# Two-layer hybrid decoder trunk: first rows in a written order, two banks for each norm transpose, another order of the mixer's parts

## The chip, the cores and the metric

The kernel runs on one core of a Trainium2 chip. The metric is the device time of one execution in microseconds; the median of three runs is compared. Engines are named as in the profile: PE is TensorE (PEld its weight loads), DVE is VectorE, ACT is ScalarE, POOL is GpSimd, SP is SyncE, which here issues almost all DMAs.

## The reference, cut to what matters

Two layers, each of them three sublayers with a norm behind each. `mod` are nine rows of 1024 per layer that depend on `c` alone: shift, scale and gate for each sublayer.

```python
for l in range(DEPTH):                       # DEPTH 2, SEQ 256, D_MODEL 1024, D_FF 2816
    mod = (silu(c) @ ada_w[l] + ada_b[l]).reshape(b_, 3, 3, 1024)
    y = swiglu(modulate(x, mod[:, 0, 0], mod[:, 0, 1]), ffn_w13[l, 0], ffn_w2[l, 0])
    x = layer_norm(ALPHA * x + 0.5 * (1 + mod[:, 0, 2])[:, None, :] * y, ln_g[l, 0], ln_b[l, 0])
    y = token_mixer(modulate(x, mod[:, 1, 0], mod[:, 1, 1]), w_in[l], w_out[l], ...)
    x = layer_norm(ALPHA * x + (1 + mod[:, 1, 2])[:, None, :] * y, ln_g[l, 1], ln_b[l, 1])
    y = swiglu(modulate(x, mod[:, 2, 0], mod[:, 2, 1]), ffn_w13[l, 1], ffn_w2[l, 1])
    x = layer_norm(ALPHA * x + 0.5 * (1 + mod[:, 2, 2])[:, None, :] * y, ln_g[l, 2], ln_b[l, 2])
# token_mixer: h @ w_in, then three groups of heads of width 64 side by side, then @ w_out:
#   6 heads gated delta rule (GDN): conv + silu on q, k, v; unit q, k; a scan over 4 chunks of 64 tokens
#   4 heads MoBA (one block of 256 here, so plain causal softmax attention)
#   6 heads mLSTM: conv + silu on q, k; sigmoid output gate; a norm over each head
```

All inputs and the output are float32.

## The kernel before

**Numbers.** Each float32 operand of a large product is cut into a high part `hi` (rounded to fp32r, on ACT, line 101) and a low part `lo` (the difference, on DVE, line 104), and a product is three matmuls, `mm3` (lines 108 to 111): high by high, high by low, low by high. The activations are kept transposed as `xh` and `xl`, eight blocks of 128 columns by 256 tokens.

**Stages.** Six phases run in turn: FFN, mixer, FFN in layer 0, then the same in layer 1. An FFN (`ffn`) takes the 22 column blocks of `w13` two at a time, and then `out_rows` multiplies with `w2`; the products of its last four rows are held back (`held`) and issued within the norm. Between two phases stands `boundary`: gate, residual add, statistics and scaling of the norm on DVE, ACT and POOL, then for each half `t` of the tokens two calls of `turn`, which transpose four blocks of 128 columns on PE into one bank of PSUM; `mod` applies the next scale and shift, even columns on ACT and odd ones on DVE, and `high` and `low` cut the result. The first projection of the next phase (`product`) follows for each half. The planner that orders the instructions never lets two engines use one PSUM bank at a time. The `late` items are modulation columns whose last products wait for this place.

**Orders.** Three kinds of order matter. SP's queue, and so the order of nearly all loads, is the program order. `boundary` is written by hand for PE, DVE and ACT. All else is ordered by the planner, which works down the program order by what it takes to be ready; engines then run their queues strictly in order. `tc.issue_after(ins)` ties what is traced inside it to follow `ins` on the engine of `ins`.

**The first rows.** The first FFN has no boundary ahead of it. `first_rows` (lines 559 to 618) loads all of `x`, transposes it, and then for each of eight blocks k of 128 rows loads 128 columns of `ada_w` each for shift and scale of that block (rows of 512 bytes) and 128 rows of `w13` for seven column blocks. DVE sums the products of the `ada_w` block with `sc_` (line 595 and 597, eight steps), PE sums over partitions (line 599), two adds finish shift and scale, ACT and DVE make `xh`, `xm` and `xl`, and 42 matmuls per k add into seven banks. Six parameter loads and four transposes of them stand ahead (`param_columns`), on ACT's DMA queue.

**Background.** The other modulation rows come from `ada_block`: four chunks of `ada_w`, each with two DVE steps of 128x1024, put into a list `bg` that the FFNs work off between their weight chunks; with the fourth chunk `fin()` sums over partitions on PE.

**The mixer.** `mixer` projects q, k and v of GDN (`proj_T`, `conv_silu`, squares on POOL at line 771), runs GDN's steps as a generator `gd`, adds the residual rows of the coming norm (`state["residual"]()`, lines 514 to 520, two loads of norm rows and four DVE steps of 128x1024), projects the mLSTM parts and MoBA's, and then takes turns with the generators `ml` and `mo`. GDN is a scan; its solve of the triangular blocks runs on POOL (lines 976 and 978). `mix_T` transposes the finished columns: blocks 0 to 2 are GDN, 3 and 4 MoBA, 5 to 7 mLSTM. `out_rows` multiplies with `w_out` in the block order (3, 4), (0, 1), (2, 5), (6, 7). The mLSTM output gate (`mlstm_gate`, line 830) is one Sigmoid on ACT.

## Time and profile before

| | us |
|---|---|
| median of three runs | 1236.38 |
| lowest and highest | 1231.99, 1237.64 |
| the profiled execution | 1231.17 |
| its span, first to last instruction | 1229.5 |
| PE busy in it | 1160.3 (94%) |
| DVE busy | 894.8 (73%) |
| ACT busy | 578.4 (47%) |
| POOL busy | 107.2 (9%) |
| mean granted clock of PE | 0.975 |

The profile gives, for one execution, when each instruction ran, how long its engine had been idle ahead of it and what ended that idle time. Busy shares of a whole span are means over stages with different limits, so the stretches are read by themselves. Matmuls overlap in the pipeline: the distance between their starts is their pace, not the duration shown for one.

### The profile page before, as it was taken

What the parts mean: (1) busy time and instruction counts of PE and PEld (TensorE: products, weight loads), DVE (VectorE), ACT (ScalarE), POOL (GpSimd) and SP (SyncE); (2) the same over time, 40 slices, a digit from 0 to 9 for tenths busy, and PEclk for the clock granted to TensorE, in tenths of its full rate; (3) what the DMA queues carried; (4) which work ended last, traced back from release to release, by engine and by line L of the source; (5) the groups of instructions that cost most, each with busy time, mean ns of one, the idle gap of its engine ahead of it and who ended that gap; (6) DMA issues with size and microseconds to landing.
All of it is one profiled execution on the core that took longest, in us unless ns stands there. A gap on an engine that the chain in (4) does not pass through costs nothing.

```text
span 1229.5 us, 21037 instructions
## 1 busy us (share of the span) xinstructions
PE 1160.3 (94%) x8584; PEld 1051.4 (86%) x8584; DVE 894.8 (73%) x1423; ACT 578.4 (47%) x934; POOL 107.2 (9%) x174
## 2 busy tenths in 40 slices
PE   6899999988999799999999999999999979999996
PEld 4899988788997678999778999888898867999984
DVE  7889977677665679888578877776884766756655
ACT  3355443366573355544335554435755625544431
POOL 1000000012511200000000000001332120000001
PEclk9899999989998899999999999998999989999998
DMA  9999797363342159987638977671643431765650
GB/s 307 343 320 369 277 410 292 119 184 127 122 148 85 35 191 354 325 313 291 237 140 283 365 260 280 252 275 51 209 125 126 161 113 33 258 224 178 234 206 34
DMA packets 171522, 265.99 MB, mean 216 GB/s; under 512 B 5407, under 2 KB 136987, under 8 KB 171425
## 3 DMA queue, kind: packets, MB, share of 16 engines
q1 hardware_dynamic: 170368, 262.32, 62.1%
q10 hardware_dynamic: 1056, 2.32, 0.5%
q8 instruction: 67, 1.10, 0.4%
q14 instruction: 31, 0.25, 0.1%
HBM read 263.56 MB, written 1.06 MB: 215 GB/s over the span
## 4 chain that ended last, share of the span: by engine, by line
PE 77%; DVE 8%; DMA 5%; ACT 4%; POOL 3%; issue 2%; SPq 0%; DVEq 0%; ACTq 0%; POOLq 0%
PE pg L110 14%; PE pg L109 14%; PE pg L111 14%; PE pacc L109 9%; PE pacc L111 8%; PE pacc L110 8%; DMA raw<-in_ffn_w_dram 3%; DVE lo L104 2%; PE pg L225 1%; POOL xt L976 1%; POOL X L978 1%; ACT xm L450 1%; PE pg L233 1%; ACT hi L101 1%; DMA araw<-in_ada_w_dram 1%
## 5 line engine op out<-in xcount | busy, mean ns | idle before, releaser
L104 DVE TENSOR_TENSOR lo<-raw,hi 128x1024 fp32r<-128x1024 f32 (+3 forms) x332 | 396.4, 1200 | 163.4 <-PE pg L111 73.0
L101 ACT ACTIVATE hi<-raw 128x1024 fp32r<-128x1024 f32 (+4 forms) x352 | 353.9, 1027 | 294.8 <-DMA raw<-in_ffn_w_dram 113.3
L109 PE MATMUL pg<-xh,hi 128*128 128x256 f32 x1568 | 447.6, 287 | 5.4 <-ACT xh L604 2.7
L110 PE MATMUL pg<-xl,hi 128*128 128x256 f32 x1568 | 447.6, 286 | 1.5 <-DVE xl L607 1.5
L111 PE MATMUL pg<-xh,lo 128*128 128x256 f32 x1568 | 445.7, 285 | 0.0
L109 PEld LDWEIGHTS pg<-xh,hi 128*128 128x128 f32 x1568 | 301.9, 193 | 8.1 <-ACT xh L604 3.4
L110 PEld LDWEIGHTS pg<-xl,hi 128*128 128x128 f32 x1568 | 303.7, 194 | 3.4 <-DVE xl L607 2.0
L111 PEld LDWEIGHTS pg<-xh,lo 128*128 128x128 f32 x1568 | 303.2, 194 | 0.3
L260 DVE SCALAR_TENSOR_TENSOR adacc<-araw,sc__132,adacc 128x1024 f32<-128x1024 f32 x118 | 150.9, 1279 | 4.9 <-DMA araw<-in_ada_w_dram 4.1
L110 PE MATMUL pacc<-lo,hh 128*128 128x512 f32 x352 | 139.8, 397 | 1.6 <-DVE lo L104 1.5
L109 PE MATMUL pacc<-hi,hh 128*128 128x512 f32 x352 | 140.8, 400 | 0.0
L111 PE MATMUL pacc<-hi,hl 128*128 128x512 f32 x352 | 139.6, 396 | 0.0
L110 PEld LDWEIGHTS pacc<-lo,hh 128*128 128x128 f32 x352 | 66.3, 188 | 19.4 <-DVE lo L104 3.4
L109 PEld LDWEIGHTS pacc<-hi,hh 128*128 128x128 f32 x352 | 66.3, 188 | 16.4 <-issue 0.7
L111 PEld LDWEIGHTS pacc<-hi,hl 128*128 128x128 f32 x352 | 66.3, 188 | 15.9
L177 POOL TENSOR_TENSOR lsm<-lsm,mhalf 128x1 f32<-128x1 f32 x12 | 7.9, 660 | 701.1 <-DVE lsm L349 701.1
L632 ACT ACTIVATE sg<-pg 128x256 f32<-128x256 f32 x79 | 29.5, 375 | 81.2 <-PE pg L111 77.0
L639 ACT ACTIVATE hh<-h 128x256 fp32r<-128x256 f32 x82 | 33.8, 412 | 47.2 <-DVE h L634 46.8
L640 DVE TENSOR_TENSOR hl<-h,hh 128x256 fp32r<-128x256 f32 x82 | 34.4, 420 | 19.5 <-ACT hh L639 19.5
L109 PE MATMUL pacc<-hi,xh 128*128 128x512 f32 (+1 forms) x80 | 34.1, 427 | 10.2 <-ACT xh L454 10.2
L733 DVE SCALAR_TENSOR_TENSOR cy<-pg,cvc,cy 128x255 f32<-128x255 f32 (+2 forms) x90 | 40.1, 473 | 4.2 <-ACT cy L731 3.7
L339 ACT ACTIVATE lsq<-n,lsm 128x512 bf16<-128x512 f32 x24 | 17.3, 720 | 49.3 <-DVE lsm L328 31.5
(377 smaller groups left out, 1398.8 us busy)
## 6 DMA issues: line engine op xcount, KB each, us to landing
raw<-in_ffn_w_dram SPq DMA_DIRECT2D x118, 1024.0 KB, 5.7
araw<-in_ada_w_dram SPq DMA_DIRECT2D x64, 1024.0 KB, 8.6
raw<-in_w_in_dram SPq DMA_DIRECT2D x16, 1024.0 KB
araw<-in_ada_w_dram SPq DMA_DIRECT2D x16, 512.0 KB, 6.5
raw<-in_w_out_dram SPq DMA_DIRECT2D x8, 1024.0 KB, 4.8
raw<-in_ffn_w_dram SPq DMA_DIRECT2D x16, 448.0 KB, 6.1
raw<-in_ffn_w_dram SPq DMA_DIRECT2D x14, 512.0 KB, 4.5
raw<-in_w_in_dram SPq DMA_DIRECT2D x8, 792.0 KB, 6.7
```

The costliest lines, as they stand in the source:

```text
L101: state["hi"] = nc.scalar.activation(hi, v, AF.Copy)
L104: state["lo"] = nc.vector.tensor_tensor(lo[j], v[:, j * m:(j + 1) * m, :], hi[:, j * m:(j + 1) * m, :].bitcast(F32), op=ALU.subtract)
L109: nc.tensor.matmul(o, ah, bh, start=first, stop=False)
L110: nc.tensor.matmul(o, ah, bl, start=False, stop=False)
L111: nc.tensor.matmul(o, al, bh, start=False, stop=last)
L225: nc.tensor.matmul(pt[:, m:m + 1], acc[:, m * 128:(m + 1) * 128], ones[:, 0:1], start=True, stop=True)
L260: nc.vector.scalar_tensor_tensor(acc, raw[:, kk, :], sc_[:, k:k + 1], acc, op0=ALU.mult, op1=ALU.add)
L339: return nc.scalar.activation(sq[:, :c1 - c0], self.n[:, t, c0:c1], AF.Square, bias=self.cols(t, 6), accum_out=self.cols(t, 3 + h))
L632: nc.scalar.activation(sg, pa, AF.Silu)
L639: nc.scalar.activation(hh[:, f, :], h, AF.Copy)
L640: nc.vector.tensor_sub(hl[:, f, :], h, hh[:, f, :].bitcast(F32))
L733: nc.vector.scalar_tensor_tensor(y[:, s:], ps[:, :T - s], w(3 - s), y[:, s:], op0=ALU.mult, op1=ALU.add)
```

## The change

- `first_rows` gets a written order for PE, DVE and ACT. `ada_w` for block 0 is loaded first, then `x` in two halves of columns with `w13` 0 between, then `ada_w` 1, `w13` 1; blocks 2 to 7 of `ada_w` come in pairs (rows of 1 KB, in the tiles that later hold `hh` and `hl`). DVE sums five of the eight row blocks (seven for a pair) and PE the others. `xm` moves to ACT. The empty products that opened the banks are gone.
- Five of the six parameter loads go to SP and, with three transposes, into the second weight chunk of the first FFN.
- `ada_block`: `fin()` is a fifth item of the list; the gate's bias row is loaded by SP.
- `boundary`: each `turn` takes two banks, even columns in one and odd in the other; the late columns come after the transposes of the second half.
- `mixer`: two small copies (`gt`, `gi`) and the squares move to ACT, the residual goes behind the `mqk` projections, the gate becomes Exp, add and reciprocal and comes ahead of the mLSTM heads, MoBA's heads come after mLSTM's, and the output projection takes (3, 4) last.

```diff
 def param_columns():
+            column(rows[:72, 0, :], 72, abc[:, 0:72])
+            return lambda: more_param_columns(rows)
+        def more_param_columns(rows):
+            nc.sync.dma_start(rows[0:72, 1, :], ada_b[1].rearrange("(k p) -> k p", p=128))
...
+            for i, n, dst in ((1, 72, abc[:, 72:144]), (2, 96, lnc), (3, 120, cvc)):
                 column(rows[:n, i, :], n, dst)
 def ada_block(l, blk, pool, late=None):
-                            nc.scalar.dma_start(st["acc"][0:1, :], ada_b[l:l + 1, blk * 1024:blk * 1024 + D])
+                            nc.sync.dma_start(st["acc"][0:1, :], ada_b[l:l + 1, blk * 1024:blk * 1024 + D])
-                    if i == 3 and late is None:
-                        fin()()
-                    elif i == 3:
+                    if i == 3 and late is not None:
                         late.append(fin)
-            return [chunk(i) for i in range(4)]
+            return [chunk(i) for i in range(4)] + ([lambda: fin()()] if late is None else [])
 def boundary(l, s, acc, held, late, nx, sp, bp):
             def turn(t, q):
-                pts[t, q] = v = (ps_acc(1) if t else ps_g()).rearrange("p (a b) -> p a b", a=4)
+                pts[t, q] = v = [(ps_acc(1) if t and not q else ps_g()) for _ in range(2)]
                 for k in range(4):
-                    nc.tensor.transpose(v[:, k, :], nr.n[:, t, (4 * q + k) * 128:(4 * q + k + 1) * 128], ident)
+                    nc.tensor.transpose(v[k % 2][:, k // 2 * 128:k // 2 * 128 + 128],
+                                        nr.n[:, t, (4 * q + k) * 128:(4 * q + k + 1) * 128], ident)
...
             ps = [nx["product"](0, xh, xl)]
+            turn(1, 0)
+            turn(1, 1)
             if late:
                 pt = ps_g()
                 left = [fin(pt[:, i * 8:i * 8 + 8]) for i, fin in enumerate(late)]
-            turn(1, 0)
-            turn(1, 1)
 def first_rows(l, i, nf):
+            groups = {0: 1, 1: 1, 2: 2, 4: 2, 6: 2}
+            nv = {1: 5, 2: 7}
...
+            def mod_p(k):
+                n0 = nv[groups[k]]
+                for i in range(groups[k]):
+                    for j in range(2):
+                        o, sl = cps[:, 8 * j + k + i:8 * j + k + i + 1], slice(i * 128, (i + 1) * 128)
+                        for kk in range(n0, KD):
+                            nc.tensor.matmul(o, raws[k][:, kk, j, sl], sc_[:, kk:kk + 1], start=kk == n0, stop=False)
+                        nc.tensor.matmul(o, sums[k][:, j, sl], ones[:, 0:1], start=False, stop=True)
...
+            with tc.manual_schedule(engines={E.PE, E.DVE, E.Activation}):
+                load_mod(0), load_x(0), load_w(0), load_x(1), load_mod(1), load_w(1)
+                turn(0), turn(2)
+                mod_v(0, 0, nv[1])
+                mod_p(0), mod_c(0), apply(0)
+                ws = high(0)
+                low(0, 0, ws), low_x(0), low(0, 1, ws)
+                for k in range(KD):
+                    if k + 2 in groups:
+                        load_mod(k + 2)
+                    if k + 2 < KD:
+                        load_w(k + 2)
+                    now = ws
+                    if k + 1 < KD:
+                        ws = high(k + 1)
+                    if k == 0:
+                        products(0, 0, now[0], 0, nf - 2)
+                        products(0, 1, now[1], 0, nf - 2)
+                        turn(4), turn(6)
                     else:
+                        products(k, 0, now[0])
+                    if k + 1 in groups:
+                        mod_v(k + 1, 4 if groups[k + 1] > 1 else 0, nv[groups[k + 1]])
+                        mod_p(k + 1)
+                    if k + 1 < KD:
+                        low(k + 1, 0, ws)
+                        if k + 1 in groups:
+                            mod_c(k + 1)
+                        apply(k + 1)
+                        low(k + 1, 1, ws), low_x(k + 1)
+                    if groups.get(k + 2, 1) > 1:
+                        mod_v(k + 2, 0, 4)
+                    if k == 0:
+                        products(0, 0, now[0], nf - 2)
+                        products(0, 1, now[1], nf - 2)
+                    else:
+                        products(k, 1, now[1])
 def ffn(l, i, xh, xl, nx, first=None):
+                if not first and cc == 1:
+                    more_columns()
 def mixer(l, mp, xh, xl, pz):
-                nc.vector.tensor_copy(gt[:, t, :], pz[t][:, 0:12])
+                nc.scalar.activation(gt[:, t, :], pz[t][:, 0:12], AF.Copy)
-                    nc.gpsimd.tensor_mul(r, dst, dst)
+                    nc.scalar.activation(r, dst, AF.Square)
-            state["residual"]()
             mqk = mp.tile([128, 6, T], F32, tag="mqk", name="mqk")
...
             proj_T(2316, [(0, 1), (2, 3), (4, 5)], mqk_sink)
+            with tc.issue_after(state["silu"].ins):
+                state["residual"]()
...
             def mlstm_gate():
-                with tc.issue_after(state["exp"].ins):
-                    state["exp"] = nc.scalar.activation(state["so"], state["so"], AF.Sigmoid)
+                so = state["so"]
+                with tc.issue_after(state["after"]):
+                    nc.scalar.activation(so, so, AF.Exp, scale=-1.0)
+                nc.vector.tensor_scalar(so, so, 1.0, None, op0=ALU.add)
+                nc.vector.reciprocal(so, so)
...
             next(ml)
-            for _ in mo:
-                pass
+            mlstm_gate()
             next(ml)
-            mlstm_gate()
...
-            mix_T(mix, mh, mlo, [(3, 5, 0, 2)], ps_mb)
             mix_T(mix, mh, mlo, [(0, 3, 0, 1), (0, 3, 1, 2)], ps_d)
             for _ in ml:
                 pass
+            for _ in mo:
+                pass
             mix_T(mix, mh, mlo, [(5, 7, 0, 2), (7, 8, 0, 2)], ps_d)
+            mix_T(mix, mh, mlo, [(3, 5, 0, 2)], ps_mb)
...
-                    rest = end(*out_rows(lhs, w_out[l], [(3, 4), (0, 1), (2, 5), (6, 7)], nx))
+                    rest = end(*out_rows(lhs, w_out[l], [(0, 1), (2, 5), (6, 7), (3, 4)], nx))
```

## Rows read from the trace of the kernel before

**Rows 1.** The page, part 4: shares of the span on the chain by engine.

```profile
PE 77%; DVE 8%; DMA 5%; ACT 4%; POOL 3%; issue 2%; SPq 0%; DVEq 0%; ACTq 0%; POOLq 0%
```

**Rows 2.** Stretches: length, busy (instructions) of PE, PEld, DVE, ACT, POOL; PE clock, DMA share, GB/s.

```profile
22.50:74.00 51.50, 47.22 (x347) 46.72 (x348) 44.93 (x97) 22.39 (x27) 0.00 (x0) 0.93 1.05 332
74.00:223.00 149.00, 148.01 (x998) 135.03 (x997) 129.84 (x149) 66.33 (x97) 0.96 (x1) 1.00 0.90 330
80.00:90.00 10.00, 10.00 (x85) 10.00 (x85) 10.00 (x14) 6.33 (x11) 0.00 (x0) 1.00 0.97 356
```

**Rows 3.** What PE waited for: total us, times, longest us.

```profile
PE pgdn L301 <- DVE mix L1239: 11.9, 2, 6.0
PE pacc L109 <- ACT xh L454: 10.2, 10, 1.4
PE pm L773 <- POOL sq L771: 5.6, 4, 1.9
...
PE pg L233 <- DVE adacc L260: 2.5, 1, 2.5
```

**Rows 4.** Timeline of the first rows: start, us, instruction [idle before, what ended it].

```profile
10.71 0.35 DVE L595 TENSOR_SCALAR ada<-araw,sc__132 128x256 f32<-128x256 f32 x1 [4.21 <-DMA araw<-in_ada_w_dram]
...
17.64 0.95 ACT L101 ACTIVATE hi<-raw 128x896 fp32r<-128x896 f32 x1 [2.76 <-DMA raw<-in_ffn_w_dram]
...
22.53 0.58 PE L110 MATMUL pg<-xl,hi 128*128 128x256 f32 x1 [0.89 <-DVE xl L607]
...
54.38 0.95 ACT L101 ACTIVATE hi<-raw 128x896 fp32r<-128x896 f32 x1 [4.28 <-DMA raw<-in_ffn_w_dram]
...
73.85 0.64 ACT L632 ACTIVATE sg<-pg 128x256 f32<-128x256 f32 x2
```

**Rows 5.** Groups by line and shape: busy us, mean ns | idle before.

```profile
L104 DVE TENSOR_TENSOR lo<-raw,hi 128x896 fp32r<-128x896 f32 x16 | 17.4, 1089 | 2.6 <-PE pacc L111 2.2 <-issue 0.3
...
L604 ACT ACTIVATE xh<-xT,modc 128x256 fp32r<-128x256 f32 x8 | 4.8, 599 | 8.5 <-DVE modc L602 8.5
...
L597 DVE SCALAR_TENSOR_TENSOR ada<-araw,sc__132,ada 128x256 f32<-128x256 f32 x56 | 25.7, 479 | 0.4
```

**Rows 6.** Stretches with other row sizes of the loads, columns as in rows 2.

```profile
90.00:110.00 20.00, 20.00 (x168) 20.00 (x167) 19.70 (x26) 9.99 (x16) 0.00 (x0) 1.00 1.05 369
150.00:180.00 30.00, 30.00 (x197) 26.84 (x196) 25.93 (x32) 12.78 (x18) 0.00 (x0) 1.00 1.02 408
```

**Rows 7.** Timeline of the fourth boundary, DVE and PE.

```profile
834.18 0.41 DVE L448 TENSOR_SCALAR xm<-pg,sp,bp 128x128 f32<-128x128 f32 x1 [0.79 <-ACT xm L450]
...
839.08 0.45 PE L109 MATMUL pacc<-hi,xh 128*128 128x396 f32 x1 [1.05 <-ACT xh L454]
```

**Rows 8.** Timeline in the first mixer, ACT and DVE on two banks of `pg`.

```profile
387.45 0.28 ACT L1210 ACTIVATE nds<-pg 128x130 f32<-128x130 f32 x1 [2.62 <-PE pg L1209]
...
387.46 0.28 DVE L1204 SCALAR_TENSOR_TENSOR mP<-pg,Wx 128x128 f32<-128x128 f32 x1
```

**Rows 9.** Timeline at the start of the first mixer, DVE and ACT.

```profile
265.07 2.36 DVE L518 TENSOR_TENSOR xa<-n,gb 128x1024 f32<-128x1024 f32 x2 [0.52 <-DMA gb<-in_ln_g_dram]
...
271.68 2.00 ACT L101 ACTIVATE hi<-raw 128x1024 fp32r<-128x1024 f32 x2 [6.70 <-DMA raw<-in_w_in_dram]
```

**Rows 10.** Timeline at the end of the first mixer, PE.

```profile
415.09 1.09 PE L301 MATMUL pgdn<-ident,mix 128*128 128x128 f32 x4 [5.98 <-DVE mix L1239]
```

**Rows 11.** The stretch behind it, columns as in rows 2.

```profile
417.00:419.20 2.20, 2.20 (x7) 1.64 (x6) 0.44 (x2) 0.00 (x0) 0.00 (x0) 0.50 0.00 0
```

**Rows 12.** Timeline in the first mixer, MoBA's second pair of heads: first scores, last output.

```profile
376.44 0.79 PE L1250 MATMUL pmb<-bqk 64*128 64x128 f32 x2
...
386.46 0.74 DVE L1285 TENSOR_TENSOR mix<-pm,bsm 128x256 f32<-128x256 f32 x2
```

**Rows 13.** Two lines with a reciprocal: duration ns min/median/max, first and last start us, form.

```profile
L881 DVE RECIPROCAL be__2579<-be__2579 x1: 228/228/228, 256.5 to 256.5; 128x12 f32<-128x12 f32 x1
...
L1222 DVE RECIPROCAL mrd<-mrd x4: 180/182/182, 397.4 to 997.4; 128x6 f32<-128x6 f32 x4
```

126 lines of the change are left out of this document (69 added, 57 removed).

## The prediction

> **What bounds the kernel now.** I read the chain of waits first: 77% of the span hangs on TensorE (PE) [rows 1]. So a microsecond is won only where PE waits or runs at its low clock. The stretches say where to look: from 74 to 223 us PE is busy 148.0 of 149 us at full clock, while from 22.5 to 74 us, the first rows of the first FFN, it is busy 47.2 of 51.5 us, with DMA at a share of 1.05 [rows 2]. The list of what PE waited for shows four items that this change touches: the last mixer output (11.9 us in two waits), `xh` at the norms (10.2 us in ten), the squares of `gdn_sink` (5.6 us in four) and one gate row of `ada_block` (2.5 us) [rows 3]. The large products themselves stay as they are. The rest goes part by part, against the profiled run of 1231.17 us (span 1229.5); the median of the runs shown, 1236.38, is 5.2 us above it, which I add at the end.
>
> **Part A, first rows.** *What is removed.* The first `ada_w` columns reach VectorE (DVE) at 10.71 us, yet full triples of products run only from 22.53 us, where PE had waited for `xl`; the last of the eight weight slices reaches ScalarE (ACT) at 54.38 us, and the stage ends at 73.85 us, when the first Silu follows its last product [rows 4]. The stage has 336 products of 256 columns; in a full stretch 85 of them take 10 us [rows 2], 0.12 us each, so 40.3 us are needed and 51.3 are taken. The start is late by order: `x` stands before the `ada_w` columns, and DVE has eight multiply-adds of 479 ns and two splits of 1089 ns in its queue for each slice [rows 5].
>
> *What is new.* The eight DVE steps become five for slices 0 and 1 (three go to PE as small products) and seven of double width for each of the pairs 2, 4, 6. In a run of them a step advances by about 0.41 us, and by about 0.7 at double width (less than twice, as a part of it is fixed): 64 steps of 26 us become 31 of 19. DVE's `xm` goes to ACT.
>
> *DMA.* Six slice loads separate 17.64 from 54.38 us, 6.12 us for each 1.97 MB [rows 4]. Rows of 4 KB move at 408 GB/s [rows 6], and I count the 3.5 KB weight rows as these: 2.25 us for 0.92 MB, which leaves 3.87 us for a 1.05 MB block of 512-byte `ada_w` rows. The stretch at 369 GB/s is half 1 KB and half 4 KB rows [rows 6], so 1 KB rows come to 3.1 us a block. Six blocks in pairs save 0.76 us each, 4.6 us.
>
> *Start.* Counted back from 17.64 us the stream begins at 3.9 us. In the new order `ada_w` 0 lands at 7.8, half of `x` at 9.1, `w13` 0 at 10.2 to 11.3 us. Five DVE steps (2.1), small products and adds (0.9), `xh` and `xm` (0.6 each [rows 5]), the first high half (0.95), its low half (1.1) and `xl` (0.4) put the first full triple at 14.5 instead of 22.5 us.
>
> *Middle.* Pair 2 lands at 24.9 us; seven double steps, the column products, `xh` and `xl` take 8 us, so slice 2 starts at 33 us. PE reaches the middle of slice 1 at about 25.5 and waits there 4 to 5 us, as the rest of slice 1 stands behind `mod_p(2)` in PE's written order. Pairs 4 and 6 land at 35.6 and 46.3, ahead of need. Six slices of 5.05 us from 33 us end at 63.3, and 1.2 more for the low clock behind the wait makes 64.5: 9 us gained (5 to 12: the low end is a start and a pair 2 us later each, the high end no wait at the pair). The FFN behind can pass it on: PE sets its pace and its DMA share is 0.90 [rows 2].
>
> The Trainium skill speaks against part of this: "DMA: Bandwidth & Descriptors", section Specifications, puts transfers of 512 B or more at line rate. By that the pairs move no faster than single blocks. The 332 GB/s of this stage [rows 2] beside the two rates of [rows 6] say otherwise. What the sum would be is the second rival.
>
> **Part B, the gate's own step.** `fin()` becomes a fifth item of the background list, one slot behind the last chunk, with a weight chunk of products between. In the third FFN PE then doesn't wait 2.5 us for DVE's last multiply-add [rows 3]; with a little low clock behind it I count 3 us (1 to 3.5). The bias row goes from ACT's DMA queue to SP's: 4 KB, and its memset is done long before SP reaches it, so no load behind it is held.
>
> **Part C, the norms' own banks.** With all four columns of a turn in one PSUM bank, ACT and DVE read in turns: DVE's step at 834.18 starts where ACT's ended [rows 7]. With even and odd columns in two banks each engine has its own; on two banks they did read within 10 ns of each other [rows 8]. Four steps of 0.45 us become two, 0.9 us less for each quarter. The ten waits for `xh` are two a boundary, 1.0 us each on average [rows 3]. For t = 0 the 0.9 us covers the first (1.05 us at 839.08 [rows 7]): 4 us over five boundaries. For t = 1 `xh` is 0.45 us earlier and DVE's chain before it as well, and in three boundaries the late columns' products now stand between the transposes and their use, less a new wait for the scaled rows: 0.6 us each, 3 together. Sum 7 (3 to 9; the low end if only the first wait goes).
>
> **Part D, early mixer.** The residual's two row loads (1 MB, 2.6 us at 408 GB/s) and its four DVE steps (2.36 us for the first two, the others alike) stand in front of the next projection, and ACT waited 6.7 us for weights until 271.68 [rows 9]. They move behind the `mqk` projections. The queueing context around them names an ACT instruction and they run on SP and DVE, so program order alone moves them. They come back while GpSimd solves the triangular blocks, where DVE has room, or in front of that chain (the low end). The squares change from GpSimd to ACT, which saves a change of engine: 0.5 of the 1.4 us of each of four waits [rows 3]. Both mixers: 5 us (-1 to 9).
>
> **Part E, tail of the mixer.** PE waited 5.98 us for the last mLSTM rows [rows 10] and then had 2.2 us at a granted clock of 0.50, its 1.2 GHz level [rows 11], 6.0 + 1.1 us a mixer. With MoBA emitted last and (3, 4) last in the output projection, MoBA's PE work and 36 products of 512 columns (0.235 us, 8.5 us in all) can cover that chain. What is late next is MoBA: its second pair of heads takes from 376.44 to 386.46 us [rows 12]; I leave 1.5 us of it exposed. The gate costs more than it looks: Sigmoid on ACT becomes Exp, an add and a DVE reciprocal of 128x768. A reciprocal of 12 columns takes 228 ns, one of 6 takes 180 [rows 13]: 8 ns a column, 6.3 us if the slope holds, and about 1 us if it goes like the double steps of part A. I take 6.3, the slope being that operation's own rows. DVE does nothing else meanwhile, and the GDN scan needs DVE in each of its steps; I count 4 us of it on the path. Net 7.1 - 1.5 - 4 = 1.6 us a mixer, 3 for two (-8 to 13).
>
> The Trainium skill, "VectorE: DVE Perf Modes" (Walkthrough: the 8-slice pipeline in each mode), describes reciprocal as an iterative divide with a repeat count of 8. An estimate by that page is the upper end.
>
> **Part F, small loads.** Five parameter loads and three transposes move from before the start into the second weight chunk. There they queue behind megabytes on SP, and PE may wait for the transposes: -1 us (-4 to 0).
>
> **Sum.** 9 + 3 + 7 + 5 + 3 - 1 = 26 us off 1231.2: 1205 us for a profiled run, and with 5.2 us for the median 1210 us.
>
> **Rivals.**
> 1. *The reciprocal is covered.* It falls into a hole of DVE and the tail closes wholly: E is 13 and not 3, 1200 us. For it: DVE is not the bound in the mixer; against: the scan's DVE steps are short and frequent, and 6.3 us fit no gap. Chance 0.17.
> 2. *Pairs no faster.* Pair 2 lands 1.6 us later, 4 and 6 by 3.1 and 4.6; PE waits 1.6 + 1.4 + 1.5 us more, part A is 4.5: 1215 us. For it: the page's rule; against: the rates. Chance 0.13.
> 3. *The mixer's moves do nothing*, as the planner puts moved steps back, or MoBA's chain ends as late as mLSTM's did: D and E are 0, 1218 us. Chance 0.10.
> 4. *Slower.* MoBA last is exposed: two pairs of 10.0 us less 8.5 us of cover, on top of the reciprocal's 6.3, are 17.8 us against 7.1 saved, and 2 us of low clock behind such a stall: 12.7 us a mixer, 25 for two. The other parts are worth 23, so it decides from 11.5 us a mixer on; with D at -1 it gives 1245 us. For it: a pair's chain crosses PE, DVE and ACT six times; against: the output products are ready long before. Chance 0.05.
>
> **How the numbers follow.** The forecast has 0.55 (1203 to 1218 us), the rivals the rest. The unknown costs are independent, so their ends don't add; 1193 to 1228 takes in rivals 1 to 3 with their spread and leaves out less than 2 in 10. A measurement of this kernel can tell about 0.5% from no change: faster is under 1230.2, slower over 1242.6. Rival 4 and low ends that fall together give 0.04 slower and 0.07 within; 0.89 faster.
>
> **What would show it.** A: first full triple near 14.5 us, first Silu near 64.5. B: no wait at the gate row. C: ACT and DVE columns that start together, no wait of 1 us before `xh`. D: no 6.7 us wait of ACT behind the boundary. E: a reciprocal near 6 us, a last wait under 2 us before the output transposes. I am wrong if the GDN scan ends later by the whole reciprocal, or if a DMA wait before 223 us eats the gain of A.

## The result, and the profile after

The changed kernel takes 1251.05 us (median of 4 runs, 1247.99 to 1252.76), the kernel before beside it 1234.18 us: ratio 1.0139, 95% interval 1.0118 to 1.0161. It is 17 us **slower** where 26 us less were forecast. The profiled execution took 1247.99 us, its span 1246.3 us, 16.8 us above the span before. The ratios leave out two slow executions, one of ten of e13 (2807.41 us) and one of eight of e17 (1236.26 us).

Where the 17 us lie is read from one landmark: the DVE step that adds the gate at a boundary (`n<-pacc,gate`, four of them a boundary). The stretch from the fourth step of a boundary to the first of the next is a phase, the four steps themselves are the boundary. Differences of starts in the two timelines, us:

| stretch | before | after | difference |
|---|---|---|---|
| start to the first gate step (first FFN) | 223.95 | 234.99 | +11.0 |
| five boundaries, sum | 59.88 | 53.96 | -5.9 |
| first mixer | 184.30 | 185.97 | +1.7 |
| second mixer | 175.78 | 189.12 | +13.3 |
| the other three FFNs, sum | 567.81 | 564.56 | -3.3 |
| all | | | +16.9 |

Times of stages below are each read from one profiled execution. The executions of one kernel lie up to 14 us apart (e5: 1227.41 to 1241.50), so a difference of a few us in one stage counts only where several kernels or the medians show it too.

So the norms did what was forecast, and the first FFN and the mixers did the opposite. Of the 11.0 us of the first FFN 2.8 lie ahead of its first Silu (73.85 and 76.66 us) and 8.2 behind it (150.10 and 158.33 us). The chain that ended last (page, part 4) answers to [rows 1]: PE keeps 77%, DVE has 10% instead of 8.

```profile
PE 77%; DVE 10%; DMA 4%; issue 3%; ACT 3%; POOL 3%; SPq 0%; DVEq 0%; ACTq 0%; POOLq 0%
```

What PE waited for in the changed kernel (total us, times, longest) answers to [rows 3]: the 11.9 us for the mLSTM rows are gone, those for `xh` fell from 10.2 to 1.3 us, and those for the squares from 5.6 (POOL) to 3.4 us (now on ACT). Conv steps (`cy`), mLSTM weights (`mP`) and a `w2` weight stand in their place.

```profile
PE pg L109 <- DVE cy L815: 9.5, 3, 5.2
PE pg L1294 <- DVE mP L1291: 6.0, 2, 4.7
...
PE pm L855 <- ACT sq L853: 3.4, 2, 1.7
PE pacc L109 <- ACT hi L101: 3.3, 1, 3.3
```

**First rows.** Stretches of the changed kernel (columns as in [rows 2]) and its timeline (as [rows 4]):

```profile
22.50:76.66 54.16, 49.95 (x379) 49.27 (x378) 39.82 (x56) 25.16 (x35) 0.00 (x0) 0.91 0.92 322
30.00:36.50 6.50, 4.16 (x24) 4.07 (x23) 4.12 (x7) 0.00 (x0) 0.00 (x0) 0.71 1.08 372
16.50:33.20 16.70, 13.29 (x89) 12.71 (x89) 12.13 (x21) 6.52 (x9) 0.00 (x0) 0.99 1.07 368
```

```profile
16.47 0.58 PE L109 MATMUL pg<-xh,hi 128*128 128x256 f32 x1 [2.35 <-ACT hi L643]
17.93 0.58 PE L110 MATMUL pg<-xl,hi 128*128 128x256 f32 x1 [0.88 <-DVE xl L651]
...
26.28 0.16 DVE L629 SCALAR_TENSOR_TENSOR modc<-pacc,abc 128x1 f32<-128x1 f32 x1 [4.05 <-PE pacc L625]
...
28.52 4.69 DVE L615 SCALAR_TENSOR_TENSOR ada<-awide,sc__132,ada 128x512 f32<-128x512 f32 x6
...
33.27 0.59 PE L625 MATMUL pacc<-ones,ada 128*128 128x1 f32 x2 [2.35 <-DVE ada L615]
...
62.21 1.29 DVE L264 SCALAR_TENSOR_TENSOR adacc<-araw,sc__132,adacc 128x1024 f32<-128x1024 f32 x1 [1.65 <-DMA araw<-in_ada_w_dram]
...
66.21 0.39 PE L110 MATMUL pg<-xl,hi 128*128 128x256 f32 x1 [1.51 <-DVE xl L651]
...
76.66 0.64 ACT L712 ACTIVATE sg<-pg 128x256 f32<-128x256 f32 x2
```

The first Silu comes at 76.66 us, not at 64.5. The loads did not hold PE: from its first product on no wait ends with one, and from 16.5 to 33.2 us they move 368 GB/s, against 332 over the stage before [rows 2]. PE waits at 33.27 us for DVE's six double steps of the first pair, and at 66.21 us for an `xl` that stands behind a step of the background list in DVE's queue.

**The list of the first FFN.** SP's queue at its end, before (first two rows) and after, and then the changed kernel's PE:

```profile
204.08 1.14 SPq L82 DMA_DIRECT2D araw<-in_ada_w_dram  x2
209.29 0.37 SPq L82 DMA_DIRECT2D raw<-in_ffn_w_dram  x1
```

```profile
210.40 11.53 SPq L82 DMA_DIRECT2D araw<-in_ada_w_dram  x3
222.03 0.41 SPq L82 DMA_DIRECT2D raw<-in_ffn_w_dram  x1
...
230.45 0.54 PE L109 MATMUL pacc<-hi,hh 128*128 128x512 f32 x1 [3.31 <-ACT hi L101]
```

Before, two `ada_w` chunks stand ahead of the last `w2` weight, and it is issued at 209.29. After, three stand there, SP is held 11.5 us by them, the weight is issued at 222.03 and PE waits 3.31 us for its `hi`.

**Boundary.** Timeline of the fourth boundary, ACT and DVE, the answer to [rows 7]:

```profile
841.22 0.81 ACT L454 ACTIVATE xm<-pg,bp,sp 128x128 f32<-128x128 f32 x2 [2.27 <-PE pg L443]
...
841.33 0.73 DVE L452 TENSOR_SCALAR xm<-pg,sp,bp 128x128 f32<-128x128 f32 x2 [0.29 <-PE pg L443]
```

The two engines now read side by side, two columns each in 0.8 us, and the wait of 1.05 us for `xh` does not come.

**Mixers.** Both whole mixers of the changed kernel, and in the second the stretch from 2 us ahead of the first `S,WT` product of the GDN scan to the last one; then the reciprocal in it:

```profile
246.97:432.94 185.97, 173.52 (x1555) 157.60 (x1554) 128.10 (x253) 97.20 (x194) 40.01 (x63) 0.90 0.36 116
844.48:1033.60 189.12, 172.46 (x1555) 157.22 (x1554) 127.32 (x253) 97.34 (x195) 41.86 (x63) 0.90 0.35 114
...
973.31:996.47 23.16, 18.43 (x131) 15.28 (x129) 17.82 (x28) 5.88 (x11) 5.54 (x5) 0.75 0.28 91
```

```profile
982.63 4.94 DVE L919 RECIPROCAL so<-so 128x768 f32<-128x768 f32 x1
...
988.17 0.69 PE L1294 MATMUL pg<-vc,mP 128*128 128x65 f32 x2 [4.73 <-DVE mP L1291]
```

PE waits 4.73 us for the DVE step queued behind the reciprocal, and PE's mean clock over the mixer is 0.90, before 0.93 and 0.95. The same stretch of the scan took 12.91 us at clock 1.00 in the second mixer before:

```profile
964.89:977.80 12.91, 12.91 (x125) 10.43 (x124) 9.02 (x23) 7.87 (x17) 2.35 (x3) 1.00 0.38 139
```

### The profile page after: what moved, and what is told of

It reads as the page before. It is cut to its first block, busy times and chain, and to the rows that moved or that the text cites. A ratio compares the mean times of both kernels' runs of the same rounds, so it can differ in the third digit from the quotient of the medians.

```text
span 1246.3 us, 21066 instructions
## 1 busy us (share of the span) xinstructions
PE 1177.2 (94%) x8625; PEld 1074.7 (86%) x8625; DVE 895.0 (72%) x1370; ACT 580.8 (47%) x962; POOL 99.9 (8%) x162
## 3 DMA queue, kind: packets, MB, share of 16 engines
q10 hardware_dynamic: 684, 2.15, 0.5%
## 4 chain that ended last, share of the span: by engine, by line
PE 77%; DVE 10%; DMA 4%; issue 3%; ACT 3%; POOL 3%; SPq 0%; DVEq 0%; ACTq 0%; POOLq 0%
PE pg L109 14%; PE pg L110 14%; PE pg L111 14%; PE pacc L109 8%; PE pacc L110 8%; PE pacc L111 8%; DVE lo L104 2%; PE pg L229 2%; POOL X L1065 1%; DMA araw<-in_ada_w_dram 1%; DMA raw<-in_ffn_w_dram 1%; PE pg L237 1%; POOL xt L1063 1%; DVE so L919 1%; DVE cy L815 1%
## 5 line engine op out<-in xcount | busy, mean ns | idle before, releaser
L104 DVE TENSOR_TENSOR lo<-raw,hi 128x1024 fp32r<-128x1024 f32 (+3 forms) x316 | 378.8, 1206 | 150.1 <-PE pacc L110 65.1
L109 PE MATMUL pg<-xh,hi 128*128 128x256 f32 x1568 | 453.0, 289 | 14.9 <-DVE cy L815 9.3
L101 ACT ACTIVATE hi<-raw 128x1024 fp32r<-128x1024 f32 (+2 forms) x336 | 338.2, 1030 | 273.6 <-DMA raw<-in_ffn_w_dram 94.7
L109 PEld LDWEIGHTS pg<-xh,hi 128*128 128x128 f32 x1568 | 306.7, 196 | 16.7 <-DVE cy L815 9.5
L110 PEld LDWEIGHTS pg<-xl,hi 128*128 128x128 f32 x1568 | 306.9, 196 | 4.5 <-DVE xl L651 3.3
L111 PEld LDWEIGHTS pg<-xh,lo 128*128 128x128 f32 x1568 | 306.5, 196 | 2.7 <-DVE lo L104 2.3
L714 DVE TENSOR_TENSOR h<-sg,pg 128x256 f32<-128x256 f32 x79 | 32.6, 414 | 11.0 <-ACT sg L712 7.1
```

Source lines behind the costliest of these rows:

```text
L101: state["hi"] = nc.scalar.activation(hi, v, AF.Copy)
L104: state["lo"] = nc.vector.tensor_tensor(lo[j], v[:, j * m:(j + 1) * m, :], hi[:, j * m:(j + 1) * m, :].bitcast(F32), op=ALU.subtract)
L109: nc.tensor.matmul(o, ah, bh, start=first, stop=False)
L110: nc.tensor.matmul(o, ah, bl, start=False, stop=False)
L111: nc.tensor.matmul(o, al, bh, start=False, stop=last)
L714: nc.vector.tensor_mul(h, sg, pb)
```

## Experiments: one part undone

All kernels below compute the whole of the reference. Each is timed against the kernel before on the same chip; intervals are 95%.

**e1, first rows of before in the changed kernel.** `first_rows`, the loads of `x` and `param_columns` as before:

```diff
-            return lambda: more_param_columns(rows)
...
-            with tc.manual_schedule(engines={E.PE, E.DVE, E.Activation}):
...
+            modulate(0)
```

> The changed kernel with the first rows and the parameter loads of the kernel before (parts A and F undone; the gate's own step, the banks and the mixer's new order stay). Theory 1: the first FFN lost its 11 us through the written order itself (first Silu 2.8 us later, 8.2 us more behind it up to the first gate), so this run takes them back: first Silu near 73.9 us, first gate row near 224 us, median near 1240 us. Rival: the 8.2 us behind the first rows come from the fifth background step and the bias row on SP's queue (part B), which stay here: then the first gate comes near 232 us and the median near 1248 us.

Measured: 1246.91 us, ratio 1.010 (1.0061 to 1.0138); first Silu 76.46, first gate step 232.41. Most of the 11 us stays without the new first rows, 5.9 of them behind the first Silu (155.96 us from there to the gate step): the rival is right.

**e2, mixer of before in the changed kernel:**

```diff
-            nc.scalar.activation(r, dst, AF.Square)
+            nc.gpsimd.tensor_mul(r, dst, dst)
...
-            mix_T(mix, mh, mlo, [(3, 5, 0, 2)], ps_mb)
```

> The changed kernel with the whole mixer of the kernel before (parts D and E undone). Theory: the mixers alone lose 15 us against before (1.7 in the first, 13.3 in the second), so this run comes to about 1236 us, with the PE wait of 6 us ahead of the last mLSTM rows back in both mixers. Rival: the second mixer's 13 us come from what precedes it (late loads of the background list, another order that the planner finds), and stay: about 1248 us.

Measured: 1256.67 us, 1.0173 (1.0138 to 1.0207), mixers 189.9 and 194.0. Neither was expected: the old mixer text is slower here than the new one, and 6 and 18 us slower than the same text in the kernel before.

**e3, banks, late columns and gate's own step on the kernel before:**

```diff
-            return [chunk(i) for i in range(4)]
+            return [chunk(i) for i in range(4)] + ([lambda: fin()()] if late is None else [])
...
-                pts[t, q] = v = (ps_acc(1) if t else ps_g()).rearrange("p (a b) -> p a b", a=4)
+                pts[t, q] = v = [(ps_acc(1) if t and not q else ps_g()) for _ in range(2)]
```

> The kernel before with the norms' own banks and the gate's own step alone (parts B and C). Theory: parts add up; the five boundaries are 6 us shorter (0.1 + 1.6 + 1.3 + 1.3 + 1.6) and the third FFN and its followers 3 us, so 1225 to 1229 us against 1234. Rival: the gain of the banks is only there because something else of the change frees an engine at the boundary, or the fifth step delays the first FFN by 8 us: 1233 to 1240 us.

Measured: 1251.51 us, 1.0139 (1.0099 to 1.0178): first gate step 231.81, boundaries 54.6 us, but mixers 191.0 and 188.9, though no line of the mixer is edited. What changed is PE's order, which the planner makes anew: in e2 and e3 144 projection products stand ahead of the first `g,tri` product of GDN in both mixers; before there are 135 and 90, in the changed kernel 113 and 113. So parts do not add up by themselves, and single parts had to be tried with an eye on that order.

**e4, one Sigmoid as gate in the changed kernel:**

```diff
-                with tc.issue_after(state["after"]):
-                    nc.scalar.activation(so, so, AF.Exp, scale=-1.0)
-                nc.vector.tensor_scalar(so, so, 1.0, None, op0=ALU.add)
-                nc.vector.reciprocal(so, so)
+                with tc.issue_after(state["exp"].ins):
+                    state["exp"] = nc.scalar.activation(state["so"], state["so"], AF.Sigmoid)
```

> The changed kernel with one Sigmoid on ACT as gate again, behind the mLSTM heads' first step; MoBA stays last, the projection takes (3, 4) last, the squares stay on ACT. Theory: the DVE reciprocal of 128x768 (4.95 us in the trace) stands on the path in the second mixer (PE waits 4.7 us for a copy behind it) and partly in the first: 5 to 8 us come back, about 1244 to 1246 us. Rival: the scan and MoBA's chain set the end and the reciprocal only fills a hole of DVE: 1249 to 1252 us.

Measured: 1240.30 us, 1.0047 (1.0022 to 1.0072), 11 us less than the changed kernel and more than the 5 to 8 expected; mixers 178.8 and 186.0, with 7.2 and 3.1 us less. The scan, from its first `S,WT` product to its last, comes back by 7.7 and 7.4 us, so the reciprocal costs more there than its 4.95 us; in the second mixer 3.6 us are lost again ahead of the scan.

## Experiments: one part alone

**e5, new first rows on the kernel before** (the diff of `first_rows`, `param_columns` and the loads, nothing else).

```diff
+            with tc.manual_schedule(engines={E.PE, E.DVE, E.Activation}):
+                load_mod(0), load_x(0), load_w(0), load_x(1), load_mod(1), load_w(1)
...
+                if not first and cc == 1:
+                    more_columns()
```

> The kernel before with the new first rows and the moved parameter loads alone (parts A and F); the mixers keep PE's order of the kernel before (135 and 90 projection products ahead of the first `g,tri` product of GDN). Theory: the written order loses by itself, as the pairs' DVE steps and small products stand in PE's way: first Silu near 76.7 us, first gate row 3 to 5 us later than before, median 1237 to 1240 us. Rival: the loss seen in the changed kernel came from the gate's own step and the lists of the background, not from the first rows; alone they gain: first Silu 66 to 72 us, median 1226 to 1231 us.

Measured: 1235.22 us, 1.0008 (0.9979 to 1.0037): no difference in the median. In the profiled execution (1238.10 us) the first Silu comes at 76.90 and the first gate step at 228.80, as the theory has them. Over all runs the first Silu comes between 71.64 and 76.46 us in twelve kernels with the old first rows and between 73.79 and 77.31 us in seven with the new ones: about the same. Behind it the moved small loads do show: from the first Silu to the first gate step e5 takes 151.90 us, and the other two kernels with the new rows and without the gate's step (e15, e17) 153.40; the nine with neither take 149.66 to 150.10. In e5 PE waits there for the moved transposes:

```profile
91.37 0.32 PE L188 MATMUL pg<-ident,rows 120*128 120x120 f32 x1 [1.68 <-DVE abc L189]
```

All seven kernels with the new rows have this wait, of 1.31 to 1.95 us.

**e6, two banks a turn alone:**

```diff
+                pts[t, q] = v = [(ps_acc(1) if t and not q else ps_g()) for _ in range(2)]
...
+                    nc.tensor.transpose(v[k % 2][:, k // 2 * 128:k // 2 * 128 + 128],
```

> The kernel before with two banks for each turn alone (half of part C; the late columns keep their place). PE's order of the mixers comes out as 90 products ahead of the first `g,tri` product in the first mixer (135 before) and 144 in the second (90 before). Theory: the place that the planner finds for GDN's first product sets the length of the mixer: first mixer about 176 us (184.3 before), second about 189 us (175.8 before), five boundaries 4 to 6 us shorter, sum near 1234 us. Rival: the mixers' times hang on something else of the changed kernel (loads, position in the run): 184 and 176 us as before, and the boundaries' gain stands whole, 1226 to 1229 us.

Measured: 1227.67 us, 0.9956 (0.9937 to 0.9976). Boundaries 6.3 us shorter; mixers 177.5 and 187.8, near the expected 176 and 189. The stages of the profiled run sum to 2.5 us less than before, the medians differ by more (5 us). PE at GDN's start, first mixer, then second:

```profile
260.81 0.61 PE L887 MATMUL pgdn<-g__2580,tri 128*128 128x6 f32 x4 [0.26 <-DVE g__2580 L879]
262.20 1.16 PE L896 MATMUL pgdn<-tri,ge 128*128 128x128 f32 x8
...
858.59 0.61 PE L887 MATMUL pgdn<-g__8720,tri 128*128 128x6 f32 x4 [1.12 <-DVE g__8720 L879]
862.89 2.93 PE L896 MATMUL pgdn<-tri,ge 128*128 128x128 f32 x12 [3.69 <-DVE ge L891]
```

The first product stands 25.3 us behind the fourth gate step (235.50) in the first mixer and 32.7 us behind it (825.93) in the second, and there PE also waits 3.69 us for `ge`.

**e7, the new tail of the mixer alone** (gate, MoBA last, (3, 4) last):

```diff
-            for _ in mo:
-                pass
+            mlstm_gate()
             next(ml)
...
             for _ in ml:
                 pass
+            for _ in mo:
+                pass
```

> The kernel before with the new tail of the mixer alone (part E: gate by Exp, add and reciprocal and ahead of the heads, MoBA last, (3, 4) last); the starts of the mixers stay at 135 and 90 products. Theory: the closing wait of 6.0 us and its 1.1 us of low clock go, the reciprocal's 4.95 us come in their place, 0 to 3 us gained a mixer: first mixer 182 to 185, second 173 to 177 us, median 1229 to 1234 us. Rival: MoBA last is exposed besides: a mixer 3 to 8 us longer, 1240 to 1250 us.

Measured: 1234.88 us, 1.0020 (1.0000 to 1.0040): the closing wait is gone, and nothing is won: mixers 183.5 and 182.7, 0.8 us shorter and 6.9 longer than before.

**e8, banks and that tail with one Sigmoid** (e6, and e7 without its gate).

```diff
             next(ml)
-            for _ in mo:
-                pass
             next(ml)
             mlstm_gate()
...
-                    rest = end(*out_rows(lhs, w_out[l], [(3, 4), (0, 1), (2, 5), (6, 7)], nx))
+                    rest = end(*out_rows(lhs, w_out[l], [(0, 1), (2, 5), (6, 7), (3, 4)], nx))
```

> The kernel before with two banks for each turn, MoBA last and (3, 4) last, and the gate's one Sigmoid on ACT as before. PE's order of both mixers comes out as 90 products ahead of the first `g,tri` product. Theory: order, banks and tail are each worth what the stages show: first mixer 176 less 5 us for the closing wait (171), second 171 us, boundaries and the FFNs behind 6 to 9 us shorter: 1203 to 1210 us. Rival: MoBA last costs what it saves: mixers near 176 us both, 1217 to 1220 us; or the start's order does nothing: 184 and 176 less the tail, 1217 to 1222 us.

Measured: 1217.97 us, 0.9872 (0.9834 to 0.9911), mixers 178.7 and 179.5. The first rival holds: MoBA last gives back what the closing wait saved. In the first mixer (PE):

```profile
388.46 0.55 PE L1276 MATMUL pmb<-ident,bP 128*128 128x128 f32 x3
...
402.33 0.39 PE L1284 MATMUL pm<-vb,bPT 128*128 128x64 f32 x2
403.23 0.33 PE L301 MATMUL pmb<-ident,mix 128*128 128x128 f32 x1 [0.52 <-DVE mix L1287]
```

For 15 us, from 388.5 to 403.2, MoBA's heads run through PE, ACT and DVE in turns with few output products between them (7 in all).

**e9, the gate's own step alone:**

```diff
-                    if i == 3 and late is None:
-                        fin()()
-                    elif i == 3:
+                    if i == 3 and late is not None:
                         late.append(fin)
...
+            return [chunk(i) for i in range(4)] + ([lambda: fin()()] if late is None else [])
```

> The kernel before with the gate's own step alone (part B: `fin()` as a fifth item of the list, the bias row on SP's queue). PE's order of the mixers comes out as 90 products ahead of the first `g,tri` product in the first and 135 in the second, the reverse of before. Theory 1: 24 items of the first FFN's list become 28, the last `ada_w` chunks slide behind the last weights, and the first gate row comes 6 to 9 us later, near 231 us. Theory 2: the mixers' times follow their orders: first 176 to 180 us, second 181 to 184 us. Sum 1233 to 1240 us. Rival to 1: the late columns' new place does the 8 us, first gate row near 224 to 226 us. Rival to 2: position counts, 184 and 176 us.

Measured: 1240.40 us, 1.0060 (1.0030 to 1.0090); first gate step 232.72, 156.58 us behind the first Silu against 150.10 before. Theory 1 holds. SP, ACT and PE at the end of its first FFN:

```profile
208.12 10.83 SPq L82 DMA_DIRECT2D araw<-in_ada_w_dram  x3
219.05 0.88 SPq L82 DMA_DIRECT2D raw<-in_ffn_w_dram  x1
...
227.06 3.52 ACT L101 ACTIVATE hi<-raw 128x1024 fp32r<-128x1024 f32 x4 [13.95 <-DMA raw<-in_ffn_w_dram]
...
228.17 0.79 PE L109 MATMUL pacc<-hi,hh 128*128 128x512 f32 x1 [3.31 <-ACT hi L101]
```

ACT stood 13.95 us for the weight behind the three chunks. Theory 2 falls in part: the mixers came to 180.1 (90 products) and 178.2 (135), so here 135 is no slower than 90. In the kernel before and in e5 it was (184.3 against 175.8, 180.9 against 179.5). Over all runs the seven mixers with 144 products took 184.5 to 194.0 us, those with 90 171.9 to 182.7.

**e10, the early mixer alone** (part D):

```diff
-                nc.vector.tensor_copy(gt[:, t, :], pz[t][:, 0:12])
+                nc.scalar.activation(gt[:, t, :], pz[t][:, 0:12], AF.Copy)
...
+            with tc.issue_after(state["silu"].ins):
+                state["residual"]()
```

> The kernel before with part D alone (residual behind the `mqk` projections, squares and two small copies on ACT). PE's order comes out as 113 products ahead of the first `g,tri` product in both mixers. Theory: with the small copy on ACT the products of GDN's start come later than at 90 and the squares wait in ACT's queue: first mixer 178 to 186, second 183 to 188 us, median 1233 to 1242 us. Rival (the prediction): 2.5 us gained a mixer, 182 and 173 us, 1229 us.

Measured: 1231.89 us, 0.9992 (0.9976 to 1.0009): nothing, under the range of the theory and above the rival; mixers 178.9 and 179.6.

**e11, banks and the squares on ACT, tail of before:**

```diff
-                    nc.gpsimd.tensor_mul(r, dst, dst)
+                    nc.scalar.activation(r, dst, AF.Square)
```

> The kernel before with two banks for each turn, and the squares of GDN on ACT; the tail is that of before. PE's order comes out as 90 products in both mixers. Theory: the tail with MoBA last (sigmoid gate) gains nothing over the tail before, so this run is as fast as the banks with that tail: mixers 176 to 180 us each, boundaries 6 us shorter, 1214 to 1221 us. Rival: the tail with MoBA last is worth its 6 us of wait a mixer and only the starts were slower there: 1226 to 1230 us here.

Measured: 1216.10 us, 0.9872 (0.9851 to 0.9892), mixers 177.9 and 175.9. The theory holds, and e8's finding with it: with 90 products in both, the old tail is as fast as the new one, as long as the squares' move is worth nothing by itself, which no run tries alone.

## Experiments: towards the cause, and a faster kernel

**e12, e8 with half of MoBA early.** `moba` yields behind its second head:

```diff
+                if h == 1:
+                    yield
...
             next(ml)
+            next(mo)
+            next(mo)
             next(ml)
             mlstm_gate()
```

> The kernel before with two banks for each turn, the gate's one Sigmoid, two of MoBA's four heads ahead of the mLSTM heads and two last, (3, 4) last in the output projection. PE's order comes out as 90 products in both mixers. Theory: in the tail with all of MoBA last, two pairs of heads run nearly alone on PE behind the mLSTM rows (388 to 404 us of the first mixer), which ate the 6 us that the closing wait gave back; with one pair last the output products cover it: 3 to 6 us less a mixer, 173 to 176 us, 1205 to 1213 us. Rival: the planner or the chain of one pair gives the wait back: 1216 to 1222 us.

Measured: **1205.08 us** (1204.45 to 1207.20), 0.9783 (0.9762 to 0.9804), faster than both kernels; mixers 172.1 and 171.9.

**e13, e12 with the late columns moved:**

```diff
+            turn(1, 0)
+            turn(1, 1)
             if late:
...
-            turn(1, 0)
-            turn(1, 1)
```

> The kernel with two banks, the Sigmoid gate and half of MoBA last (the run before it that came to 1205 us), and in addition the late columns behind the second half's transposes (the other half of part C). PE's order turns from 90 to 144 products ahead of the first `g,tri` product in both mixers; nothing else of the mixers is edited. Theory: that order alone makes a mixer 8 to 14 us longer (172 to 180 or 186), the boundaries and the FFN behind them gain 1 to 3 us: 1219 to 1231 us. Rival: the order of the start costs nothing where the tail is mended, and what made such mixers slow was the tail: 1202 to 1207 us.

Measured: 1231.64 us, 0.9987 (0.9963 to 1.0010), mixers 185.5 and 184.4. No line of the mixer differs from e12; the order that the planner makes anew costs 13 us each. Of these 8 and 9 us lie ahead of the first `g,tri` product, the rest behind it.

**e14, e12 with the reciprocal** (and the gate ahead of the mLSTM heads' second step):

```diff
-                    state["exp"] = nc.scalar.activation(state["so"], state["so"], AF.Sigmoid)
+                    nc.scalar.activation(so, so, AF.Exp, scale=-1.0)
+                nc.vector.tensor_scalar(so, so, 1.0, None, op0=ALU.add)
+                nc.vector.reciprocal(so, so)
```

> The kernel with two banks and half of MoBA last, with Exp, add and DVE reciprocal as gate, ahead of the mLSTM heads, instead of the one Sigmoid. Theory: the 4.95 us of DVE stand in front of the heads' DVE steps and the GDN scan, 4 to 7 us a mixer (176 to 179 us each; the start of the second comes out at 112 products besides, 0 to 3 us): 1213 to 1222 us. Rival: DVE has the room with MoBA's heads spread, and the reciprocal is hidden: 1203 to 1208 us.

Measured: 1222.20 us, 0.9910 (0.9878 to 0.9943), mixers 181.8 and 179.7: 9.7 and 7.8 us more for an instruction of 4.95. In the second mixer 112 products and no longer 90 stand ahead, so part of its loss may be that order. The whole mixers of e12, e13 and e14, two rows each, and then the scan of the first mixer, cut as in the section on the result, e12 and e14:

```profile
234.19:406.26 172.07, 165.30 (x1554) 151.89 (x1553) 121.10 (x256) 96.49 (x185) 42.97 (x69) 0.94 0.39 125
818.30:990.23 171.93, 164.82 (x1555) 150.56 (x1554) 121.37 (x255) 96.34 (x185) 42.98 (x69) 0.94 0.39 125
```

```profile
236.46:421.91 185.45, 171.97 (x1555) 158.29 (x1554) 121.05 (x256) 96.72 (x185) 43.97 (x69) 0.90 0.37 116
832.72:1017.17 184.45, 171.06 (x1555) 157.81 (x1554) 121.76 (x255) 97.32 (x185) 42.70 (x69) 0.90 0.37 117
```

```profile
235.58:417.36 181.78, 172.47 (x1554) 156.65 (x1553) 125.94 (x258) 95.22 (x184) 42.59 (x69) 0.91 0.38 118
828.72:1008.42 179.70, 168.33 (x1555) 153.63 (x1554) 127.19 (x257) 95.08 (x184) 45.01 (x69) 0.92 0.39 120
```

```profile
361.48:377.76 16.28, 16.28 (x144) 13.20 (x143) 10.76 (x31) 7.79 (x20) 2.90 (x4) 1.00 0.29 100
362.79:386.87 24.08, 22.38 (x141) 17.87 (x140) 17.79 (x36) 6.61 (x19) 3.63 (x4) 0.71 0.21 70
```

The same matmuls keep PE busy for 165 us at a mean clock of 0.94 (e12) and for 171 to 172 us at 0.90 (e13): of its 13 us about half is PE idle, the other half PE busy for longer at the lower clock. In e14 7.8 of the 9.7 us lie in the scan: 1.7 us of PE idle, the rest PE busy for longer at a clock of 0.71 instead of 1.00. From the first `S,WT` product to the last, nine of the ten scans in the five kernels with the reciprocal ran at a mean clock of 0.63 to 0.82, and 24 of the 28 scans in the fourteen without it at 1.00. So the reciprocal brings the low clock with it, but is not the only thing that does.

**e15, the changed kernel without the gate's own step** (the diff of e9, reversed).

```diff
-            return [chunk(i) for i in range(4)] + ([lambda: fin()()] if late is None else [])
+            return [chunk(i) for i in range(4)]
```

> The changed kernel without the gate's own step (part B undone, all else as changed; 113 products in both mixers as there). Theory: the first FFN takes its 6 to 9 us back, as the list has 24 items again: first gate row near 227 us, median 1241 to 1246 us, the mixers unchanged at 186 and 189 us. Rival: with the new first rows the list runs late by itself, first gate row 232 to 235 us, median 1248 to 1252 us.

Measured: 1240.28 us, 1.0061 (1.0037 to 1.0084); first gate step 227.19, 7.8 us earlier than in the changed kernel. Of these 4.9 lie behind the first Silu (153.40 us from there, 158.33 in the changed kernel), the rest ahead of it. The theory holds for the first FFN, the median is a little under its range; the mixers came to 189.8 and 185.3, 4 us up and 4 down.

**e16, the changed kernel with one Sigmoid and half of MoBA early** (the diffs of e4 and e12; the gate stands behind the heads' second step).

```diff
-                nc.vector.reciprocal(so, so)
...
+            next(mo)
+            next(mo)
```

> The changed kernel with one Sigmoid as gate and half of MoBA ahead of the mLSTM heads; all else as changed. Theory: the mixers' loss is the tail's (reciprocal and MoBA last), so they come to 172 to 178 us although PE's order stays at 113 products; with the first FFN's 8 us still lost 1222 to 1230 us. Rival: the start at 113 products and the squares on ACT hold the second mixer at 184 us or more: 1234 to 1240 us.

Measured: 1223.08 us, 0.9924 (0.9899 to 0.9949), mixers 174.1 and 174.3, though 113 products stand ahead: 12 and 15 us less than in the changed kernel. The tail is what made its mixers long.

**e17, e16 and e15 together:**

```diff
-            return [chunk(i) for i in range(4)] + ([lambda: fin()()] if late is None else [])
+            return [chunk(i) for i in range(4)]
...
-                nc.vector.reciprocal(so, so)
```

> The changed kernel with all that was found to cost undone: the gate's own step out of the list, one Sigmoid as gate, half of MoBA ahead of the mLSTM heads. First rows, banks, late columns, squares, copies and residual stay as changed. Theory: the account is closed; 1223 us of the run with the mended tail less the 8 to 11 us that the list cost: 1212 to 1216 us, first gate row near 227 us, mixers 172 to 176 us. Rival: the two repairs overlap, as the late loads of the first FFN were partly hidden behind something else: 1218 to 1224 us.

Measured: 1227.01 us, 0.9924 (0.9900 to 0.9948): the account does not close. Behind the first Silu the list's step gives back what it did in e15 (153.40 us), but the first Silu comes at 77.31 and so the first gate step at 230.70. And the second mixer comes to 188.4 us against 174.6 of the first, with the same text. The scan of the second mixer in e16 and in e17, from 2 us ahead of its first `S,WT` product to the last ones:

```profile
964.12:978.69 14.57, 14.57 (x135) 11.88 (x135) 9.41 (x29) 8.09 (x21) 2.35 (x3) 1.00 0.21 73
```

```profile
963.73:986.58 22.85, 22.85 (x134) 18.86 (x134) 9.02 (x28) 5.78 (x16) 2.35 (x3) 0.63 0.13 47
```

Nearly as many matmuls, PE busy throughout in both, and 8.3 us between them: the granted clock is 0.63, mostly the 1.2 GHz level. Ahead of it PE had waited 2.15 us for `U` (until 958.42); in e16 no such wait stands there. That the wait brought the clock down is argued from its place, not tried. The eight executions spread from 1217.45 to 1236.26 us, and the profiled one took 1229.76: whether the fastest, which comes near the theory, had this slow scan isn't shown.

## Why the prediction was wrong, point by point

Three steps failed most. Part B counted the wait that its fifth item saves, and not the loads that it moves (e9). Part E put 4 us of the reciprocal on the path and left 1.5 us of MoBA exposed, where one Sigmoid and half of MoBA early in their place save 12 and 15 us a mixer (e16). And no term stood for the planner's order of the mixers, which a step of part C turns (e13, 13 us a mixer). Part A's gain was eaten within its own rows.

- **Part A (9 us gained; 0 measured).** The middle failed: slice 2 starts at 40.34 us and not at 33. The first full triple came at 17.93 us instead of 14.5, as PE waited 2.35 us for the first `hi`, which ACT makes after `xh` and `xm`. The pair's double steps begin only at 28.0 us: DVE had waited 4.05 us for the column sum of slice 1, which PE's written order puts behind products of slice 0, and then had `lo` and `xl` of slice 1 to make. The steps take 0.79 us each (4.69 for six), not 0.7, and PE goes on at 36.27. Left out were the second half of slice 1, which by the prediction's own words stood behind that wait (2.5 us at full clock, 4.07 here), and the small products of the other two pairs (47.90 to 49.60 and 59.76 to 61.46, 1.7 us each). Left out too was the background list on DVE: with the wait at 66.21 and the lower clock behind it half a slice takes 5.77 us (64.32 to 70.09), where 2.52 is the time at full clock (52.20 to 54.72). Rival 2, pairs no faster, is not what set the end, as no wait of PE from the first product on ends with a load; how fast rows of 1 KB are by themselves no run shows. The Trainium skill's rule on 512 B ("DMA: Bandwidth & Descriptors", Specifications) is neither borne out nor refuted by any of this.
- **Part B (3 gained; 5 to 6.5 lost behind the first Silu, by e15 and e9).** The step "one slot behind the last chunk" counted the wait saved and not that 24 items became 28: three loads fell into the last slot, ahead of a weight on SP's queue. The prediction looked at what the bias row is moved past on SP and not at what the list moves. The gain itself did not come either: the 2.5 us [rows 3] are gone in the third phase (the second FFN), but 13.7 us earlier in it PE now waits 1.48 and 1.70 us. All seven kernels with the gate's step have these two waits, and the others keep one of 2.0 to 2.6 us.

```profile
480.82 0.38 PE L109 MATMUL pg<-xh,hi 128*128 128x256 f32 x1 [1.48 <-ACT hi L101]
...
483.03 0.39 PE L111 MATMUL pg<-xh,lo 128*128 128x256 f32 x1 [1.70 <-DVE lo L104]
```

- **Part C (7 gained; 5.9 at the boundaries).** Right in mechanism and size. What it missed is that it turns the planner's order of the mixers: the late columns from 90 to 144 products in both (e13), the banks by themselves to 90 and 144 (e6).
- **Part D (5 gained; nothing, e10).** Near the low end of its range. The residual's DVE steps came to lie among the conv steps of GDN's second projections, the first of them waits 4.18 us for its row load, and PE waits there, in the first mixer of the changed kernel:

```profile
285.93 2.36 DVE L522 TENSOR_TENSOR xa<-n,gb 128x1024 f32<-128x1024 f32 x2 [4.18 <-DMA gb<-in_ln_g_dram]
290.17 2.03 DVE L523 TENSOR_TENSOR xa<-xa,gb 128x1024 f32<-128x1024 f32 x1
292.52 1.21 DVE L523 TENSOR_TENSOR xa<-xa,gb 128x1024 f32<-128x1024 f32 x1
...
297.62 0.58 PE L109 MATMUL pg<-xh,hi 128*128 128x256 f32 x1 [5.17 <-DVE cy L815]
298.22 0.86 ACT L101 ACTIVATE hi<-raw 128x792 fp32r<-128x792 f32 x1 [6.99 <-DMA raw<-in_w_in_dram]
```

  The 6.70 us of ACT [rows 9] did not go: behind the boundary ACT now waits 2.01 us (276.7), and 6.99 us at 298.22.
- **Part E (3 gained; about 27 us between the changed kernel and e16).** The reciprocal was sized well (6.3 against 4.95 us) and its place was named, but "4 us of it on the path" failed: 8 to 10 us a mixer (e14), as the scan then runs at the low clock. The Trainium skill's iterative divide with a repeat count of 8 ("VectorE: DVE Perf Modes", Walkthrough: the 8-slice pipeline in each mode) was taken as the upper end without a figure, and the measured 4.95 us lies under the 6.3 of the slope. "1.5 us of MoBA exposed" failed as well: e8 shows 15 us of MoBA at the end, and e12 that half of it early is worth 7 us a mixer. That is rival 4, which had 0.05; its argument, a chain that crosses three engines, was the better one. Its price was too high: 12.7 us a mixer against the kernel before, where e7, the same tail alone, lost 6.9 us in the second mixer and none in the first. That its 1245 us lies near the measured time is luck, since it still counted the gains of parts A and B.
- **Part F (1 lost; about 2 to 3).** Right in mechanism and within its range: PE waits for the moved transposes, and the stretch behind the first Silu is 1.8 us longer in e5 and 3.3 in e15 and e17.
- **The range** took the parts as independent. They are tied by the planner: 13 us a mixer hang on an order that edits elsewhere turn. And e17 shows 14 us between two mixers of one text, both with 113 products ahead, half of it in the scan at the low clock. No term stood for either. Open is which cost makes the planner put the products ahead; it was not tried.

## What to carry to other kernels

Where a planner orders the work, compare the order of the stages that the edit does not touch as well, before any time is summed: late columns moved at the boundaries cost 26 us in two mixers (e13). A step added to a list that is shared out over slots moves everything that hangs on the list, loads first. For a chain of small matmuls, count the clock: a long DVE instruction in front of it costs its own time and then the slower chain behind it (e14; for a wait alone this is only argued, e17); spreading an independent chain in two halves around it (e12) won what moving it whole did not.
